# Fourier layer of a hybrid diffusion block on Trainium2: sixteen operand buffers, gate rows ahead of the last transposes, the transform's sums on VectorE

## The chip, the cores and the metric

The kernel runs on one core of one Trainium2 chip. The metric is the time of one execution on the device, in microseconds (us). Three executions of the kernel before took 2755.8, 2761.44 and 2761.8 us; their median is 2761.44 us. The profiled execution took 2763.41 us, of which the profile's span covers 2761.6 us.

## The reference

Two layers work on 2048 latent tokens of width 1024, with 256 context tokens. Layer 0 is attention and is not touched, apart from two loads at its start. Its output projection and the Fourier layer after it are what the change rearranges:

```python
def fourier_layer(x, shift, scale, gate, norm_g, w_in, w_out):
    h = modulate(x, norm_g, shift, scale)
    u, g = jnp.split(h @ w_in, 2, axis=-1)
    uf = u.reshape(b, n, F_GROUPS, F_GROUP_DIM)          # 4 groups of 256 channels
    f = jnp.fft.fft2(uf, axes=(1, 3), norm="ortho").real.reshape(b, n, F_WIDTH)
    return x + gate * ((f * jax.nn.silu(g)) @ w_out)
# ... and the final rms_norm(x, final_g)
```

All is in fp32 to a close tolerance, so every product is made of three matmuls of split operands: a high part (fp32r) and the rest (high by high, low by high, high by low).

## The kernel before

The helper `mm3` (L58 to L60) issues such a triple; `split` (L49, L51, L54) makes the two parts: a cast on ScalarE or GpSimd, and a subtraction on VectorE (or GpSimd). The program goes through these stages:

- **Projections and attention** (to about 2007 us). The order on TensorE, VectorE and ScalarE inside attention is written out by hand. At its start SyncE's queue loads keys and values; the helper around L685 also loads raw output weights (`wol`, 256 KB each), which are split later between attention's steps.
- **Output projection 0 and second norm** (L769 to L856). For each of four groups of 512 tokens, eight operands u are formed, multiplied with resident weights (`w0h`, `w0l`), and added to x; for each block of 128 tokens `second_mod` normalises, transposes (`tr`, eight 128x128 transposes on TensorE), modulates and stores h to memory.
- **Fourier in-projection** (L862 to L1005). The work comes as eight products named by a key: gates G0, G3, G1, G2 (one for each group of 512 tokens; 192 matmuls of 512 columns each), and E0, O0, O1, E1, the even and odd folds of two token groups times the Fourier weights (O: 96 matmuls of 512 columns; E: 192 of 258 columns). Each product has eight operands h of 512 tokens, in two halves of four. The halves lie in sets of four buffers; `SETS` says which sets a product uses. There are three sets, a, b and c, that is 12 buffers. Weights come in quarters: a raw quarter (`wraw`, two buffers) is loaded by SyncE's queue, `whi` is cast by GpSimd (whose queue also mends one column of each folded operand, L916 to L922) and `wlo` subtracted by VectorE (five buffers each). Raw operands (`hraw`) have four buffers. A gate product has two halves of weights, so there are eleven changes of weights from the first product to the last.
- **Transform** (L1030 to L1094). The DFT over positions as products with cosine and sine tables (`ch`, `cl`, `sh`, `sl`), in two halves r of the output positions and four channel groups g, 24 matmuls of 256 or 258 columns for each; then sums: `g1` to `g4` on VectorE (L1072 to L1075), FM on VectorE (L1077), FL on GpSimd (L1078). The Nyquist rows Y (`pn`) come last in each half. `x` and `y` are working copies; tables for r=0 are loaded before O1, those for r=1 after E1.
- **Output projection 1 and final norm** (L1099 to L1144). All weights `w1h`, `w1l` are loaded; then for each group of tokens eight products u of FM or FL with a gate (`gl`, three buffers), the first row of four of them replaced through `gy`, `uy` and a small DMA `u<-uy`, split into `uh` and `ul`, and four blocks of 24 matmuls for each half of the columns.

A tile scheduler orders what is outside attention: it emits instructions in an order of its own and each engine's queue runs in order. SyncE's queue issues loads in order too; a load that waits for a buffer holds up those behind it.

Of the kernel before, what the change touches and what calls it, by code (L numbers as in the profile page):

```python
# [10 lines left out]
F32 = mybir.dt.float32  # L11
F32R = mybir.dt.float32r
# [23 lines left out]
NDFT = 514  # L36
# [3 lines left out]
SETS = {"G0": "ab", "G3": "ca", "E0": "bc", "O0": "ac", "G1": "ba", "O1": "cb", "E1": "ac", "G2": "ba"}  # L40
# [49 lines left out]
def block_kernel(ctx: ExitStack, tc: tile.TileContext, a):  # L90
# [29 lines left out]
    eo_d = [dt_(f"eo{ci}", [4, P, CW]) for ci in range(2)]  # L120
    s1_d = [dt_(f"s1r{g}", [4 * NG, P]) for g in range(NG)]
# [361 lines left out]
    with ExitStack() as ph:  # L483
# [191 lines left out]
        def split_weights():  # L675

            if wraw:
                l, i, lo = wraw.pop()
                hi = wop.tile([P, 512], F32R, name="woh", tag="woh")
                split(nc, hi, lo, lo.bitcast(F32), Q, Q)  # L680
                for dst, t in zip(wo_d[l], (hi, lo)):
                    ld(dst[i], t.bitcast(F32))
            for l, i, src in wouts:
                lo = wop.tile([P, 512], F32R, name="wol", tag="wol")
                ld(lo.bitcast(F32), src)  # L685
                wraw.append((l, i, lo))
                break
# [78 lines left out]
    def load_wres(gpool, pools, l, order):  # L766
# [3 lines left out]
        res = [[], []]  # L770
        for c in range(2):
            for kt in order:
                res[c].append([])
                for src, p in zip(wo_d[l], "hl"):
                    t = pools[c].tile([P, 512], F32R, name=f"w{l}{p}{kt}{c}", tag=f"{p}{kt}{c}", bufs=1)
                    ld(t.bitcast(F32), src[c * KT + kt])
                    res[c][-1].append(t)
        return res, gate

    def out_proj(pp, lp, us, wg, x, add):  # L780

        w, gate = wg
        for c in range(2):
            cs = slice(c * 512, (c + 1) * 512)
            for i in range(4):
                ps = pp.tile([P, 512], F32, name="mm", tag="mm", bufs=5)
                ts_ = slice(i * P, (i + 1) * P)
                for k in range(KT):
                    mm3(nc, ps, us[k][0][:, ts_], us[k][1][:, ts_], *w[c][k], k == 0, k == KT - 1)
# [6 lines left out]
    with ExitStack() as ph:  # L796
        pp = ph.enter_context(tc.tile_pool(name="p3ps", bufs=2, reuse_waits="tile", space=PSUM))

        up = ph.enter_context(tc.tile_pool(name="p3u", bufs=10, reuse_waits="tile"))
        w1p = ph.enter_context(tc.tile_pool(name="p3w1", bufs=1, reuse_waits="tile"))  # L800
        xp = ph.enter_context(tc.tile_pool(name="p3x", bufs=5, reuse_waits="tile"))
        lp = ph.enter_context(tc.tile_pool(name="p3l", bufs=2, reuse_waits="tile"))
        wp = ph.enter_context(tc.tile_pool(name="p3w", bufs=1, reuse_waits="tile", side="right"))
        op = ph.enter_context(tc.tile_pool(name="p3o", bufs=4, reuse_waits="tile", side="right"))
        fp = ph.enter_context(tc.tile_pool(name="p3f", bufs=2, reuse_waits="tile", side="right"))
        wres = load_wres(lp, (wp, w1p), 0, range(KT))

        def second_mod(x, t):

            xn = lp.tile([P, D], F32, name="xn2", tag="xn2")  # L810
            ln_rows(x, xn, xn)
            for b in range(2):
# [9 lines left out]

        for g in TOKEN_GROUPS:
# [30 lines left out]
            for i in out_proj(pp, lp, us, wres, xs, Q):  # L854
                st(x1_d[4 * g + i], xs[i])
                second_mod(xs[i], 4 * g + i)  # L856


    with ExitStack() as ph:
        dp = ph.enter_context(ExitStack())  # L860
# [6 lines left out]
        O4 = sp.tile([P, 4], F32, name="O4")  # L867
        tb = dp.enter_context(tc.tile_pool(name="tab0", bufs=1, reuse_waits="tile"))
        alt = tb.tile([P, NDFT], F32, name="alt")

        def load_tables(pool, r):
            c0, w = DFT_CH[r]
            out = []
            for nm in ("ch", "cl", "sh", "sl"):
                t = pool.tile([P, 4, w], F32R, name=f"{nm}{r}")
                Q.dma_start(out=t, in_=a["dft_" + nm][:, c0:c0 + w].rearrange("(j p) n -> p j n", p=P))
                out.append(t)
            return out

        with ExitStack() as pb:  # L880
            pp = pb.enter_context(tc.tile_pool(name="p4ps", bufs=4, reuse_waits="tile", space=PSUM))
            wp = pb.enter_context(tc.tile_pool(name="p4w", bufs=2, reuse_waits="tile", side="right"))
            rp = pb.enter_context(tc.tile_pool(name="p4r", bufs=4, reuse_waits="tile", side="right"))
            hp = pb.enter_context(tc.tile_pool(name="p4g", bufs=4, reuse_waits="tile", side="right"))
            cp = pb.enter_context(tc.tile_pool(name="p4c", bufs=4, reuse_waits="tile"))
            wk = pb.enter_context(tc.tile_pool(name="p4k", bufs=2, reuse_waits="tile"))
            zp = pb.enter_context(tc.tile_pool(name="p4z", bufs=1, reuse_waits="tile"))
            h34 = zp.tile([P, KT], F32, name="h34")
            h4 = zp.tile([P, KT], F32, name="h4")
            h4h, h4l = [zp.tile([P, KT], F32R, name=nm) for nm in ("h4h", "h4l")]  # L890

            def operand(src, kt, key):

                b = SETS[key][kt // 4]
                t = (cp if b == "c" else hp).tile([P, 2, G], F32R, name="hl" + b, tag="hl" + b)
                split(nc, t[:, 0, :], t[:, 1, :], src, S)
                return t[:, 0, :], t[:, 1, :]

            def load_raw(g, kt):
                raw = rp.tile([P, G], F32, name="hraw", tag="hraw")  # L900
                ld(raw, h2_d[:, kt, g * G:(g + 1) * G])
                return raw

            def load_h2(g, key):
                return [operand(load_raw(g, kt), kt, key) for kt in range(KT)]

            def load_fold(half, op, key):

                out = []
                for kt in range(KT):  # L910
                    a_, b_ = [load_raw(g, kt) for g in TOKEN_GROUPS[2 * half:2 * half + 2]]
                    e = wk.tile([P, G], F32, name="hf", tag="hf")
                    V.tensor_tensor(out=e, in0=a_, in1=b_, op=op)  # L913
                    if op is ALU.add or half == 0:

                        Q.tensor_copy(e[:, 0:1], a_[:, 0:1])  # L916
                        if half == 0 and op is ALU.add:
                            Q.tensor_copy(h34[:, kt:kt + 1], b_[:, 0:1])
                    else:

                        Q.tensor_tensor(out=e[:, 0:1], in0=b_[:, 0:1], in1=h34[:, kt:kt + 1], op=ALU.subtract)
                        Q.tensor_tensor(out=h4[:, kt:kt + 1], in0=b_[:, 0:1], in1=h34[:, kt:kt + 1], op=ALU.add)  # L922
                    out.append(operand(e, kt, key))
                return out

            def load_w4(ci):

                w = CW if ci == 0 else 512
                ph_, pl_ = [], []
                for q in range(4):  # L930
# [331 lines left out]
```

## Time and profile before

| | |
|---|---|
| median of three executions | 2761.44 us |
| profiled execution, its span | 2763.41 us, 2761.6 us |
| TensorE (PE) busy | 2588.6 us, 94% of the span |
| VectorE (DVE), ScalarE (ACT), GpSimd (POOL) busy | 1828.6, 1394.0, 1110.6 us |
| TensorE idle 2187 to 2762 us, largest | for `uh` 13.1, `whi` 10.3, `xn` 9.8, `hla` 8.4 us |

A busy TensorE is not TensorE at its peak: a matmul of 512 columns shows as 0.39 us, and the next starts 0.23 us after it, since they overlap. Where the granted clock falls to one half, the same matmuls start 0.43 us apart and TensorE still counts as busy. So the time lost in a stage is read as its length less the number of matmuls times the undisturbed spacing of their starts.

### The profile page before, as it was taken

How to read it: one execution, taken by the hardware profiler on the slowest of the kernel's cores; microseconds unless marked ns; L12 is line 12 of the kernel's file. 1: busy time of each engine (PE TensorE's matmuls, PEld its weight loads, DVE VectorE, ACT ScalarE, POOL GpSimd, SP SyncE). 2: the span in 40 equal slices, each digit the busy share in tenths (PEclk: the TensorE clock that was granted, in tenths of full speed). 3: DMA queues.
4: the chain of work that ended last, by engine and by line, in shares of the span. 5: the costliest groups of instructions: out<-in, count | busy, mean ns of one | idle time of the engine just before them, and what ended most of it. 6: DMA issues, size and time to landing. Idle time of an engine off the chain costs nothing. (4 is left out here: it accounts for less than half of the span.)

```text
span 2761.6 us, 44905 instructions
## 1 busy us (share of the span) xinstructions
PE 2588.6 (94%) x15209; PEld 2248.2 (81%) x15209; DVE 1828.6 (66%) x3959; ACT 1394.0 (50%) x3704; POOL 1110.6 (40%) x1024
## 2 busy tenths in 40 slices
PE   4889999999987999999999999999899899989798
PEld 2668887787875999999999999999878777778687
DVE  6663643756406888888888888888864534464565
ACT  3531221512215888888888888888733422221112
POOL 3221331233315996655556555566412322242000
PEclk7899999999998999999999999999999999999899
DMA  9456555466426441310151012100396766664542
GB/s 298 124 153 184 159 170 185 125 185 189 146 94 224 162 158 46 100 32 29 32 167 32 30 31 79 33 30 26 126 322 222 234 200 215 209 200 155 181 142 92
DMA packets 305621, 380.96 MB, mean 138 GB/s; under 512 B 27920, under 2 KB 188384, under 8 KB 305392
## 3 DMA queue, kind: packets, MB, share of 16 engines
q1 hardware_dynamic: 166544, 275.77, 31.3%
q10 hardware_dynamic: 133664, 93.38, 11.0%
q0 software_dynamic: 5184, 8.93, 1.1%
q8 instruction: 122, 2.00, 0.3%
q14 instruction: 107, 0.88, 0.1%
HBM read 259.39 MB, written 118.55 MB: 137 GB/s over the span
## 5 line engine op out<-in xcount | busy, mean ns | idle before, releaser
L551 DVE TENSOR_REDUCE m<-s 128x1 f32<-128x512 f32 (+1 forms) x960 | 579.7, 633 | 185.9 <-PE s L543 177.8
L563 ACT ACTIVATE e<-s,nm 128x512 f32<-128x512 f32 (+1 forms) x960 | 615.2, 654 | 68.8 <-DVE nm L555 65.5
L647 ACT CAST th<-ptr 128x512 fp32r<-128x512 f32 x576 | 340.6, 592 | 132.7 <-PE ptr L643 117.1
L651 DVE TENSOR_TENSOR tl<-ptr,th 128x512 fp32r<-128x512 f32 x576 | 379.1, 681 | 37.5 <-ACT th L647 37.5
L643 PE MATMUL ptr<-ident,e 128*128 128x128 f32 x2304 | 346.3, 273 | 8.3 <-DVE tl L651 6.8
L605 POOL TENSOR_TENSOR e<-e 128x768 f32<-128x768 f32 x189 | 343.0, 1847 | 0.0
L643 PEld LDWEIGHTS ptr<-ident,e 128*128 128x128 f32 x2304 | 269.9, 140 | 36.0 <-DVE tl L651 5.8
L543 PE MATMUL s<-kB,qh 128*128 128x512 f32 (+1 forms) x768 | 283.1, 378 | 7.3 <-ACT e L563 7.3
L51 POOL TENSOR_SCALAR whi<-wraw 128x1024 fp32r<-128x1024 f32 (+1 forms) x104 | 126.4, 1218 | 386.3 <-PE mm L59 156.1
L58 PE MATMUL mm<-whi,ghi 128*128 128x512 f32 x688 | 271.7, 398 | 10.5 <-DVE vvl L54 5.7
L60 PE MATMUL mm<-whi,glo 128*128 128x512 f32 x688 | 272.2, 397 | 3.5 <-DVE glo L54 3.5
L59 PE MATMUL mm<-wlo,ghi 128*128 128x512 f32 x688 | 272.3, 397 | 0.0
L602 POOL TENSOR_SCALAR e<-e,rs 128x768 f32<-128x768 f32 x192 | 170.5, 912 | 247.6 <-DVE rs L578 247.6
L543 PE MATMUL s<-kB,ql 128*128 128x512 f32 (+1 forms) x768 | 250.2, 338 | 0.0
L54 DVE TENSOR_TENSOR wlo<-wraw,whi 128x1024 fp32r<-128x1024 f32 (+1 forms) x104 | 134.6, 1297 | 166.6 <-POOL whi L51 166.6
L602 POOL TENSOR_SCALAR e<-e,c 128x768 f32<-128x768 f32 x189 | 168.7, 911 | 141.8 <-ACT e L563 82.1
L317 POOL TENSOR_TENSOR t<-qn,rope 128x256 f32<-128x256 f32 (+1 forms) x128 | 112.6, 901 | 261.5 <-issue 102.1
L563 ACT ACTIVATION_READ_ACCUMULATOR e<-s,nm 128x1 f32 x960 | 202.1, 211 | 0.0
L58 PE MATMUL pv<-th,vAh 128*128 128x256 f32 x576 | 168.7, 293 | 0.2 <-ACT oT L616 0.2
L58 PE MATMUL pv<-th,vBh 128*128 128x256 f32 x576 | 165.3, 287 | 0.0
L58 PEld LDWEIGHTS mm<-whi,ghi 128*128 128x128 f32 x688 | 130.5, 190 | 38.5 <-DVE vvl L54 6.1
L59 PE MATMUL pv<-tl,vAh 128*128 128x256 f32 x576 | 159.9, 278 | 0.0
(342 smaller groups left out, 6362.1 us busy)
## 6 DMA issues: line engine op xcount, KB each, us to landing
wraw<-in_w_in SPq DMA_DIRECT2D x56, 512.0 KB
hraw<-h SPq DMA_DIRECT2D x96, 256.0 KB
aw<-in_adaT SPq DMA_DIRECT2D x64, 256.0 KB
g<-sg ACTq DMA_DIRECT2D x64, 256.0 KB
gl<-g SPq DMA_DIRECT2D x64, 256.0 KB
wraw<-in_wg SPq DMA_DIRECT2D x64, 256.0 KB
kB<-kB SPq DMA_DIRECT2D x24, 384.0 KB
awr<-in_adaT SPq DMA_DIRECT2D x32, 256.0 KB
```

Of the source, the lines that this page charges most:

```text
L54: (lo_eng or nc.vector).tensor_tensor(out=lo, in0=src, in1=hi.bitcast(F32), op=ALU.subtract)
L58: nc.tensor.matmul(out, lh, rh, start=start, stop=False)
L59: nc.tensor.matmul(out, lh, rl, start=False, stop=False)
L60: nc.tensor.matmul(out, ll, rh, start=False, stop=stop)
L543: T.matmul(ps[:, c - o:c - o + cw], l, r[c // KP][:, k:k + cw], start=(j == 0), stop=(j == len(self.terms) - 1))
L551: V.tensor_reduce(out=self.m3[:, i:i + 1], in_=self.segs[i][:, 0:SEG[i][1]], axis=AX.X, op=ALU.max)
L563: S.activation(self.e[:, o:o + w], self.segs[i][:, 0:w], AF.Exp, bias=self.nm, accum_out=self.s3[:, i:i + 1])
L602: eng.tensor_scalar(out=self.e[:, sg], in0=self.e[:, sg], scalar1=by, scalar2=1.0, op0=ALU.mult, op1=ALU.mult)
L605: eng.tensor_tensor(out=onto[:, sg], in0=onto[:, sg], in1=self.e[:, sg], op=ALU.add)
L643: T.transpose(self.tr[:, k, i, :], self.p.es[i][:, kt * P:(kt + 1) * P], ident)
L647: S.copy(self.th, self.tr.rearrange("p k i q -> p k (i q)"))
L651: V.tensor_tensor(out=self.tl, in0=self.tr.rearrange("p k i q -> p k (i q)"), in1=self.th.bitcast(F32), op=ALU.subtract)
```

## The change

- `SETS` names four sets, a to d: 16 operand buffers. Sets b and d lie where later both halves' tables lie, which are loaded by GpSimd's queue once O1 and E1 are done with b and d.
- In output projection 0 the normalisation of a block is separated from its transposes, which come one block later; x has four buffers instead of five. The weights, raw and operand buffers of the in-projection are opened before the stage ends, and two of G0's eight row blocks stand ahead of the last block's transposes.
- In the transform Y comes first in each half, the FL sums move to VectorE, small copies to ScalarE, and the alternating term of the odd part moves into the sine table's row 0 (no `O4`). Row 0 of FL is replaced by Y once, by four small DMAs (and row 0 of FM by Y later, for group 2), in place of 16 loads `gy` and 16 `u<-uy`.
- In output projection 1 the first group's operands are loaded between the two halves of the weights; `gl` has five buffers; for the first group the loops are exchanged, operand by operand over four accumulators (`by_row`).
- Two of the raw output weights at attention's start wait for a VectorE copy that stands at a later step.

```diff
-SETS = {"G0": "ab", "G3": "ca", "E0": "bc", "O0": "ac", "G1": "ba", "O1": "cb", "E1": "ac", "G2": "ba"}
+SETS = {"G0": "ac", "G3": "db", "E0": "cd", "O0": "ab", "G1": "cd", "O1": "ab", "E1": "cd", "G2": "ac"}
...
                 lo = wop.tile([P, 512], F32R, name="wol", tag="wol")
+                if l == 0 and i < 2:
+                    V.tensor_copy(lo[:, 0:1], ones[:, 0:1])
                 ld(lo.bitcast(F32), src)
...
+            acc = [pp.tile([P, 512], F32, name="mm", tag="mm", bufs=bufs) for _ in range(4 if by_row else 0)]
+            for k in range(KT if by_row else 0):
+                for i in range(4):
+                    ts_ = slice(i * P, (i + 1) * P)
+                    mm3(nc, acc[i], us[k][0][:, ts_], us[k][1][:, ts_], *w[c][k], k == 0, k == KT - 1)
...
             for i in out_proj(pp, lp, us, wres, xs, Q):
                 st(x1_d[4 * g + i], xs[i])
-                second_mod(xs[i], 4 * g + i)
+                if normed:
+                    second_mod(*normed)
+                normed = norm(xs[i], 4 * g + i)
...
+        first = gates(TOKEN_GROUPS[0], "G0")
+        next(first)
+        next(first)
+        second_mod(*normed)
+        for _ in first:
+            pass
+        pa.close()
...
-            t = (cp if b == "c" else hp).tile([P, 2, G], F32R, name="hl" + b, tag="hl" + b)
+            t = (hpr if b in "ac" else hpl).tile([P, 2, G], F32R, name="hl" + b, tag="hl" + b)
...
-                e1 = rp.tile([P, G], F32, name="eo", tag="hraw")[:, 0:w]
+                e1 = gk.tile([P, 512], F32, name="eo", tag="sg")[:, 0:w]
...
-            tabs.append(load_tables(tb1, 1))
+            for r, (c0, w) in enumerate(DFT_CH):
+                tabs.append([tb.tile([P, 4, w], F32R, name=f"{nm}{r}") for nm in ("ch", "cl", "sh", "sl")])
+                for t, nm in zip(tabs[r], ("ch", "cl", "sh", "sl")):
+                    Q.dma_start(out=t, in_=a["dft_" + nm][:, c0:c0 + w].rearrange("(j p) n -> p j n", p=P))
...
-                        S.copy(y, m[:, 1, :])
...
-                        V.scalar_tensor_tensor(out=y, in0=al, scalar=O4[:, g:g + 1], in1=m[:, 1, :],
-                                               op0=ALU.mult, op1=ALU.add)
+                    S.copy(y, m[:, 1, :])
...
-                        Q.tensor_tensor(out=FL[:, g, k, rs], in0=g3[:, 0:256], in1=g4[:, 0:256], op=op)
+                        V.tensor_tensor(out=FL[:, g, k, rs], in0=g3[:, 0:256], in1=g4[:, 0:256], op=op)
...
+                        ld(FL[0:1, g, :, :], Y[g:g + 1, :, :])
...
-                gt = gp.tile([P, G], F32, name="gl", tag="gl")
+                gt = gp.tile([P, G], F32, name="gl", tag="gl", bufs=5)
...
-                if b >= 4:
-                    ld(u[0:1, :], uy[b - 4:b - 3, :])
...
+        load_c, gate = load_wres(lp, (wp, w1p), 1, KORDER)
+        w0 = load_c(0)
+        us = operands(0)
+        ld(a0_d, FM[0:1].rearrange("p g k n -> p (g k n)"))
+        wres = [w0, load_c(1)], gate
```

On TensorE, the end of output projection 0 and the start of G0 stood so before (`w0` are output weights, `xn` a normalised block, `hla` an operand of G0):

```order
L59 MATMUL mm<-w0l_25078,uh 128x512
L815 MATMUL tr<-ident,xn_26857 128x128 x4
L60 MATMUL mm<-w0h_25076,ul 128x512
L815 MATMUL tr<-ident,xn_26857 128x128 x4
L815 MATMUL tr<-ident,xn_26924 128x128 x8
L815 MATMUL tr<-ident,xn_26991 128x128 x8
L58 MATMUL mm<-hla,whi 128x512
```

In the changed kernel the last two blocks' transposes stand among G0's products:

```order
L59 MATMUL mm<-w0h_25079,ul 128x512
L57 MATMUL mm<-hla,whi 128x512
L58 MATMUL mm<-hla,whi 128x512
L59 MATMUL mm<-hla,wlo 128x512
L834 MATMUL tr<-ident,xn_26860 128x128 x4
...
L834 MATMUL tr<-ident,xn_26927 128x128 x8
...
L834 MATMUL tr<-ident,xn_26994 128x128 x4
L57 MATMUL mm<-hla,whi 128x512
L834 MATMUL tr<-ident,xn_26994 128x128 x4
```

The last block but two's transposes moved behind one triple and two, the next block's behind about ten, the last block's behind sixteen. On SyncE's queue, the loads from the transform to the first group of output projection 1 stood so before (`w1h` weights of the second half, `gl` gates):

```order
L1120 DMA gl<-g_100 128x512
L776 DMA w1h_30115<-wo1h 128x512
...
L776 DMA w1l_30145<-wo1l 128x512
L1105 DMA fing<-in_final_g 128x1024
L1113 DMA gy<-g_98 1x512
...
L1120 DMA gl<-g_97 128x512
L1136 DMA xr<-x_103 128x1024
...
L1128 DMA u<-uy 1x16x32 x2
```

They now stand so:

```order
L1147 DMA gl<-g_96 128x512
L1122 DMA F_29629<-Y_29631 1x4x1
...
L1120 DMA FL<-Y 1x16x64
L1147 DMA gl<-g_100 128x512
L1147 DMA gl<-g_97 128x512
...
L1147 DMA gl<-g_101 128x512
L779 DMA w1h_30186<-wo1h 128x512
```

All eight gates of the first group now come ahead of the weights' second half, and no `gy` or `u<-uy` is among them. On GpSimd the tables of both halves moved behind the fifth of G2's eight weight casts:

```order
L53 TENSOR_TENSOR E1L<-eo,E1H 128x258 x8
L50 TENSOR_SCALAR whi<-wraw 128x2x512 x4
L1057 DMA ch_29647<-in_dft_ch 128x4x258
...
L1057 DMA sl_29658<-in_dft_sl 128x4x256
L50 TENSOR_SCALAR whi<-wraw 128x2x512 x3
```

Before, the four of r=1 stood among the `E1L` and ahead of seven casts.

## Rows read from the trace of the kernel before

**Rows 1.** TensorE's waits, 2187 to 2762 us: in total, times, longest (us)
```profile
PE mm L58 <- ACT uh L49: 13.1, 1, 13.1
PE mm L58 <- POOL whi L51: 10.3, 6, 3.4
PE tr L815 <- DVE xn L210: 9.8, 4, 6.4
PE mm L58 <- ACT hla L49: 8.4, 4, 6.1
```

**Rows 2.** Busy time by stage: length, PE, PEld, DVE, ACT, POOL, PE clock, DMA share, GB/s
```profile
2194.50:2212.50 18.00, 8.24 (x44) 6.79 (x44) 9.54 (x27) 11.28 (x31) 4.51 (x5) 0.79 0.76 226
2212.50:2523.00 310.50, 288.65 (x1412) 237.80 (x1411) 137.33 (x176) 72.29 (x132) 87.25 (x109) 0.97 0.63 197
2523.00:2554.00 31.00, 27.23 (x217) 24.87 (x216) 23.17 (x56) 4.01 (x10) 12.60 (x20) 1.00 0.58 194
2554.00:2580.00 26.00, 10.04 (x23) 7.23 (x24) 10.58 (x20) 2.28 (x4) 3.96 (x4) 0.61 0.81 285
2580.00:2752.00 172.00, 172.00 (x746) 139.95 (x744) 107.80 (x242) 37.04 (x73) 0.00 (x0) 1.00 0.38 118
```

**Rows 3.** TensorE's timeline: undisturbed matmuls of 512 and of 256 columns
```profile
2220.00 0.40 PE L58 MATMUL mm<-hla,whi 128*128 128x512 f32 x1
2220.23 0.40 PE L59 MATMUL mm<-hla,whi 128*128 128x512 f32 x1
...
2549.88 0.28 PE L59 MATMUL ae<-cl,E1H 128*128 128x256 f32 x1
2550.00 0.28 PE L60 MATMUL ae<-ch,E1L 128*128 128x256 f32 x1
```

**Rows 4.** TensorE's timeline at the end of output projection 0
```profile
2208.01 1.94 PE L815 MATMUL tr<-ident,xn 128*128 128x128 f32 x8 [6.37 <-DVE xn L210]
2210.89 1.94 PE L815 MATMUL tr<-ident,xn 128*128 128x128 f32 x8 [0.94 <-DVE xn L210]
```

**Rows 5.** TensorE's timeline: the longest wait at a change of weights
```profile
2285.40 0.50 PE L58 MATMUL mm<-hlc,whi 128*128 128x512 f32 x1 [3.43 <-POOL whi L51]
```

**Rows 6.** SyncE's queue: raw operands in G0; gates in the transform
```profile
2271.75 9.85 SPq L901 DMA_DIRECT2D hraw<-h  x8
2535.32 17.65 SPq L1120 DMA_DIRECT2D gl<-g  x6
...
2569.95 1.21 SPq L1128 DMA_DIRECT2D u<-uy  x2
```

**Rows 7.** GpSimd's timeline ahead of the cast in rows 5
```profile
2284.16 0.18 POOL L918 COPY h<-hraw 128x1 f32<-128x1 f32 x1 [3.13 <-DMA hraw<-h]
```

**Rows 8.** TensorE's timeline at the start of output projection 1
```profile
2557.54 0.79 PE L60 MATMUL mm<-w1h,ul 128*128 128x512 f32 x1 [2.46 <-DVE ul L54]
...
2576.51 0.79 PE L58 MATMUL mm<-w1h,uh 128*128 128x512 f32 x1 [13.13 <-ACT uh L49]
```

**Rows 9.** FM sums, 2523 to 2562 us: busy us, mean ns of one, idle before
```profile
L1077 DVE TENSOR_TENSOR FM<-g,g 128x256 f32<-128x256 f32 x16 | 9.0, 593 | 0.0
```

**Rows 10.** VectorE's timeline in the transform: a sum, and two pairs of FM
```profile
2541.42 0.41 DVE L1074 TENSOR_TENSOR g<-x,bo 128x258 f32<-128x258 f32 x1
2541.75 1.30 DVE L1077 TENSOR_TENSOR FM<-g,g 128x256 f32<-128x256 f32 x2
...
2545.36 0.74 DVE L1077 TENSOR_TENSOR FM<-g,g 128x256 f32<-128x256 f32 x2
```

**Rows 11.** Start of attention: SyncE's queue, then TensorE's first scores
```profile
817.84 0.82 SPq L685 DMA_DIRECT2D wol<-in_w_out  x2
...
829.32 0.77 PE L543 MATMUL s<-kAh,qh 128*128 128x512 f32 x1 [8.79 <-issue]
```

**Rows 12.** A table's load: GpSimd's timeline at its issue
```profile
2473.46 0.78 POOL L876 DMA_DIRECT2D sl<-in_dft_sl  x1
```

**Rows 13.** The same load: KB, us from issue to landing
```profile
sl<-in_dft_sl POOLq DMA_DIRECT2D x1, 512.0 KB, 9.6
```

More of the change, by code (lines that the diff above doesn't have):

```diff
@@ new lines, in load_w4 @@
+        def load_w4(ci):
+            w = CW if ci == 0 else 512
+            ph_, pl_ = [], []
+            for q in range(4):
+                raw = wp.tile([P, 2, CW], F32, name="wraw", tag="wraw", bufs=2)[:, :, 0:w]
+                for k in range(2):
+                    kt = 2 * q + k
+                    if ci < 2:
+                        ld(raw[:, k, :], wur_d[kt][:, ci * CW:ci * CW + w])
+                    else:
+                        ld(raw[:, k, :], a["wg2"][kt * P:(kt + 1) * P, (ci - 2) * 512:(ci - 1) * 512])
+                hi = wp.tile([P, 2, CW], F32R, name="whi", tag="whi", bufs=5)[:, :, 0:w]
+                lo = wp.tile([P, 2, CW], F32R, name="wlo", tag="wlo", bufs=5)[:, :, 0:w]
+                split(nc, hi, lo, raw, Q)
+                ph_ += [hi[:, 0, :], hi[:, 1, :]]
+                pl_ += [lo[:, 0, :], lo[:, 1, :]]
+            return ph_, pl_
@@ new lines, in gates @@
+        def gates(g, key):
+            hs = [operand(load_raw(g, kt), kt, key) for kt in range(KT)]
+            for ci in (2, 3):
+                whi, wlo = load_w4(ci)
+                for i in range(4):
+                    ps = pp.tile([P, 512], F32, name="mm", tag="mm", bufs=5)
+                    ms = slice(i * P, (i + 1) * P)
+                    for kt in range(KT):
+                        mm3(nc, ps, whi[kt][:, ms], wlo[kt][:, ms], *hs[kt], kt == 0, kt == KT - 1)
+                    o = gk.tile([P, 512], F32, name="sg", tag="sg")
+                    S.activation(o, ps, AF.Silu)
+                    st(g2_d[(ci - 2) * 4 + i][:, g * G:(g + 1) * G], o)
+                    yield
@@ new lines, in gates_all @@
+        def gates_all(g, key):
+            for _ in gates(g, key):
+                pass
+        gates_all(TOKEN_GROUPS[1], "G3")
+        project(0, 0, load_fold(0, ALU.add, "E0"))
+        project(1, 0, load_fold(0, ALU.subtract, "O0"))
+        gates_all(TOKEN_GROUPS[2], "G1")
+        odd_ = load_fold(1, ALU.subtract, "O1")
+        split(nc, h4h, h4l, h4)
+        project(1, 1, odd_)
+        project(0, 1, load_fold(1, ALU.add, "E1"))
+        gates_all(TOKEN_GROUPS[3], "G2")
+        pb.close()
@@ L1024, in block_kernel @@
         FL = fp.tile([P, 4, 2, 512], F32, name="FL")
[L1025 to L1026 removed]
+        F4 = [[fp.tile([P, 4], F32, name=f"F4{b}{c}") for c in range(2)] for b in range(2)]
         Y = fp.tile([4, 2, 512], F32, name="Y")
@@ L1132, in block_kernel @@
                 us.append((h, l))
+            return us
+        load_c, gate = load_wres(lp, (wp, w1p), 1, KORDER)
[3 more added lines that the diff above has]
+        wres = [w0, load_c(1)], gate
+        fing = lp.tile([P, D], F32, name="fing", tag="fing")
+        ld(fing, a["final_g"].partition_broadcast(P))
+        for g in range(NG):
+            if g:
+                us = operands(g)
             xs = []
```

330 lines of the change are left out of this document (141 added, 189 removed).

## The prediction

> **What bounds the kernel now.** I read the stages first, then TensorE's waits, then its timeline at the longest of them, then the queues of the engine that released each. The reader should see in the waits [rows 1] that four releasers make up 41.6 us after 2187 us, and in the stages [rows 2] that all of it lies before 2580 us: from there to 2752 us TensorE is busy 172.00 of 172.00 us. TensorE is the bound, so a stage's loss is its length less its matmuls times their undisturbed spacing: 0.23 us from start to start for 512 columns and 0.12 for 256 [rows 3]. That counts the clock as well, which idle time costs: the granted clock was 0.79 and 0.61 in the two disturbed stretches and 1.00 around them [rows 2].
>
> Three stretches lose time.
>
> *End of output projection 0*, 2194.5 to 2212.5 us: 18.0 us. The order shows 12 matmuls left (2.7 us) and 32 transposes; eight take about 0.8 us at full clock (my estimate from 1.94 us at half clock, overlap taken off), so 3.2 us. Work is some 6, loss 12.0 us. TensorE stands 6.37 and 0.94 us for the normalised block [rows 4], with nothing else in its order.
>
> *In-projection*, 2212.5 to 2523 us: 310.5 us. 960 matmuls of 512 columns at 0.23 us are 221, 432 of 258 columns at 0.12 are 52, small products 2: 275. Loss 36 us: 21.9 us idle (310.5 less 288.65), and most of the rest 3% of clock [rows 2]. The places are changes of weights, the longest wait 3.43 us [rows 5], and E1's operands, one wait of 6.1 us of 8.4 [rows 1]. Before the first, SyncE's queue held eight raw operands for 9.85 us, waiting for buffers [rows 6], and GpSimd stood 3.13 us for one of them, with the late cast `whi` next in its queue [rows 7]: operands that find no buffer hold up weights behind them. E1's operands stood in set a, which the product just ahead of it still used.
>
> *Transform and start of output projection 1*, 2523 to 2751.9 us: 228.9 us. 216 matmuls at 0.12 are 25.9, 768 at 0.23 are 176.6: 202.5. Loss 26.4 us. 13.13 us is one wait for `uh` and 2.46 one for `ul` [rows 8]. Behind the first lies SyncE's queue, which stood 17.65 us at six `gl` loads with three buffers, so that half of the weights, then `gy`, then `u<-uy` at 2569.95 us came late [rows 6].
>
> **The change part by part.**
>
> *Attention's start.* Two loads of 256 KB leave the head of SyncE's queue; the first scores come 11.5 us after them, after an idle 8.79 us [rows 11]. At the 285 GB/s of a stretch dense with loads [rows 2] 0.5 MB is 1.8 us; some of it lies beside work that ends later anyway. I take 1.3 us, bounds 0 and 3. The copy they wait for is one column on VectorE, covered.
>
> *Transposes one block later, two G0 rows ahead.* 16 triples (11 us) now lie between the output weights' end and the last block's transposes. Blocks came at 2208.01 and 2210.89 us [rows 4], about 7 and 10 us after the weights' end; the order asks for them 7 and 11 us after it. So the 12.0 us fill with G0's work, if its weights and operands are there. Their loads now come ahead of the stage's end; the raw operand buffers are four, x buffers fall from five to four, and the last x load sits between raw operands, so a quarter of weights can be 3 to 5 us late. Residual 3 us, bounds 1 and 9: gain 9.
>
> *Sixteen buffers.* E1 (sets c, d) no longer follows a product on the same set except through G1, a whole O1 (22 us) earlier, so most of the 8.4 us for `hla` goes. For weight changes nothing is added to `whi`, `wlo` or `wraw` (5, 5, 2): what helps is that operands find buffers sooner, so that weights behind them on SyncE's and GpSimd's queues stand free. Following the eleven changes through both queues in the new order with durations of this trace, I find each raw quarter issued 0 to 2 us before it must be. That is thin, so I leave a third of the loss: 12 us, bounds 2 and 25. Gain 24. Where this cover goes, the next thing late is again the cast `whi`, then E1's stored halves, which now have two buffers instead of four and load in the same queue.
>
> *Tables.* Eight loads, 4.2 MB, stand on GpSimd's queue behind the fifth of G2's eight casts. Issuing one holds GpSimd 0.78 us [rows 12], so 6.2 us, between a cast that is early by half of G2 and one that must wait for a buffer of the first half's last row block. I cost them at nothing. The last of four landed after 9.6 us [rows 13]; twice the bytes, by the same row, 19 us, ends before G2's end if issued in G2's first half. The Trainium skill has a rule against me here, in "DMA: Bandwidth & Descriptors", section "Issuing engines are not separate DMA queues": transfers share the same 16 engines whoever issues them, so a second queue gives the tables no room of their own. The slow 9.6 us for 0.5 MB beside SyncE's loads agrees; it is a rival below.
>
> *Transform.* VectorE takes 16 FL sums, loses four `y` sums. A sum takes 0.41 us and the next starts 0.33 after it; a pair of FM 0.74 us alone and 1.30 beside GpSimd's FL [rows 10], on average 0.593 us each [rows 9]. With GpSimd silent I take 0.335 for each: r=0, a group is nine of them, 3.02 us, against TensorE's 24 x 0.12 = 2.88; r=1, eight, 2.68; Y five more, 1.7 us. Sum 24.5 us against TensorE's 25.9, so the two run level. After the last matmul VectorE has some of the last group's sums left, and `ul` of the first operand, whose FM was done long before, so output projection 1 starts about 1.4 us after TensorE's end, 27.3 us after the stage's start. By the mean of [rows 9] it would be slower: a rival. The Trainium skill speaks to it in "SBUF — State Buffer", section "Who interferes with whom": a VectorE instruction with two SBUF inputs contends with a GpSimd instruction that reads SBUF. By the rule the inflated sums go with GpSimd's; by the mean they stay. The two FM rows agree with the rule.
>
> *First group of output projection 1.* With `by_row` TensorE needs an operand each 12 x 0.2275 = 2.73 us; VectorE makes one in 1.3 us (u and ul, each twice a sum's columns, 0.66: an estimate from the same rows). Gates are all in SyncE's queue ahead of the second half of the weights, which has 4 x 8 x 3 x 0.2275 = 22 us of matmuls to land 4.2 MB (6.3 MB at 285 GB/s). `gl` with five buffers no longer stands 17.65 us. Row 0 by four loads of Y replaces 16 `u<-uy` and 16 `gy`; they wait for FL of the last group, 26 us in, with the second half's last weights behind them, needed 49 us in. Residual 3 us, bounds 1.5 and 9: gain 23.4.
>
> *Rest.* The saved and restored row 0, the alternating row in a table, copies on ScalarE (4.01 busy in 31 us [rows 2]): nothing, up to 1 us.
>
> Sum: 1.3 + 9 + 24 + 23.4 = 57.7 us. The profiled execution took 2763.4 us, 1.8 of it outside the span, and stands 2.0 us above the median of the runs: 2763.4 - 57.7 = 2705.7, on the median's scale 2703.7. I say 2704.
>
> **Rivals.**
>
> 1. *Forecast*, 2704; its own range 2692 to 2716. Chance 0.60.
> 2. *Weights stay late.* The eleven changes keep about what they lost, since `wraw` has two buffers and operands still share both queues with them, or G0 starts without its weights: the in-projection keeps 25 of 36 us and the projection's end 6 of 12. 2704 + 13 + 3 = 2720, between 2714 and 2730. For it: six waits for `whi` [rows 1] are more than those for operands. Against: [rows 6, 7], where the weights' lateness comes from the operands ahead. 0.22.
> 3. *VectorE becomes the transform's bound.* If its sums cost 0.593 us, 73 of them are 43 us against 27.3, 16 us late; with half the inflation 8. 2704 + 9 = 2713, to 2720. Against it: [rows 10], 0.74 for a pair alone. 0.09.
> 4. *Tables late.* If the shared engines give them and G2's last weights 19 us from G2's second half on, while SyncE already loads `w1h`, the transform starts up to 15 us later: 2719. For it: 9.6 us for one [rows 13], a DMA share of 0.63 through the whole in-projection [rows 2]. 0.04.
> 5. *Slower: every change of weights waits.* Through the added buffers operands are asked for earlier, and if their eight raw loads stand in the queue ahead of each quarter, each of the eleven changes waits for its last quarter some 6 us (the 9.85 us that eight raw loads held the queue [rows 6], less the 4 us that three quarters of a last row block of 24 matmuls leave), and the clock, at half for as long as in [rows 2], gives up 1.5 more: 82 us where 36 were lost. Then 2704 + 82 - 12 = 2774. It decides from 6.3 us a change, 70 us in all. The longest so far is 3.43 [rows 5]. 0.04.
> 6. *The change doesn't do what it says*: the scheduler orders loads so that the waits keep their places, 2755 to 2762. 0.01.
>
> **How the numbers follow.** About 0.2%, 5.5 us, is what a measurement of this kernel can tell from no change. Forecast and rivals 2 to 4 are all faster by more: 0.95. Within it lie rival 6 and part of 5: 0.02. Slower, the rest of 5: 0.03. The range takes rivals 1 to 4 in with their bounds, down to all residuals at their lower bounds (2 + 10 + 1.5 us better, 1.7 more at attention: 2689): 2688 to 2731.
>
> **What would show it.** In the changed profile the wait for `uh` after the transform should be under 2 us and no SyncE load of `gl` stand over 5 us; the granted clock should be 1.00 from 2195 to 2690 us apart from a few tenths; waits for `hla` should be gone and those for `whi` under 8 us in total; FM and FL pairs on VectorE should take 0.74 us; transposes should stand between G0's matmuls without a wait over 1.5 us; scores should start near 828 us. I am wrong if `whi` is a larger wait than before, if TensorE waits on `g` or `x` in the transform for more than 3 us, or if the first matmul of G0 waits for its weights.

## The result and the profile after

The changed kernel took 2721.4 us (median of four executions, 2719.19 to 2730.51) where the kernel before took 2761.62 us on the same chip (2755.8 to 2768.7): a ratio of 0.9859, with a 95% interval of 0.9827 to 0.9892. It is faster by 40 us, inside the stated range, but 17 us above the likeliest time and outside that case's own 2692 to 2716. It came out where rival 2 stood (2720). The profiled execution took 2719.19 us, its span 2717.3, 44.2 us less than before's.

The stages, from the first and last instruction of each on TensorE (us):

| | before | after | gain | forecast |
|---|---|---|---|---|
| start to the first output weights' matmul | 2007.5 | 2005.2 | 2.3 | 1.3 |
| from there to the transform's start | 515.5 | 493.7 | 21.9 | 9 + 24 |
| transform's start to the last matmul | 229.0 | 209.5 | 19.5 | 23.4 |
| behind the last matmul | 9.5 | 9.0 | 0.5 | 0 |

The stages of the changed kernel (columns as in [rows 2]) answer to that group:

```profile
2187.00:2198.50 11.50, 9.30 (x38) 7.52 (x37) 9.60 (x18) 4.03 (x12) 3.57 (x3) 0.85 0.68 234
2198.50:2498.80 300.30, 285.67 (x1427) 236.94 (x1427) 143.84 (x189) 80.03 (x156) 89.95 (x112) 0.98 0.67 210
2498.80:2525.70 26.90, 25.88 (x218) 24.91 (x216) 23.67 (x67) 8.40 (x33) 0.00 (x0) 1.00 0.72 241
2525.70:2536.00 10.30, 6.99 (x20) 5.07 (x21) 8.39 (x19) 2.80 (x5) 0.00 (x0) 0.67 0.99 330
2536.00:2707.00 171.00, 171.00 (x744) 139.43 (x744) 104.27 (x235) 37.42 (x72) 0.00 (x0) 1.00 0.43 142
```

The 11.8 us from the last output weights' matmul to G0's first (2200.7 to 2212.5 us before) are down to 0.2, the transform is at TensorE's pace, and the last 171 us are as full as before. But the in-projection still leaves TensorE 14.6 us idle, and its waits from 2187 us on (total, times, longest) say for what:

```profile
PE mm L57 <- POOL whi L50: 7.5, 4, 4.3
PE mm L57 <- DVE g L1110: 3.3, 1, 3.3
PE mm L58 <- DVE wlo L53: 2.4, 1, 2.4
PE tr L834 <- DVE xn L210: 2.2, 1, 2.2
PE mm L59 <- DVE wlo L53: 2.0, 2, 1.4
PE qtr L982 <- DVE row L1017: 1.6, 1, 1.6
PE mm L57 <- ACT uh L48: 1.0, 1, 1.0
PE mm L57 <- POOL hf L970: 0.8, 1, 0.8
```

Against [rows 1], the 13.1 us for `uh` are 1.0 and the 8.4 us for `hla` have gone; the waits for weights, `whi` and `wlo`, are 11.9 us and have not. (`hf` is the mend that ended just behind a cast in GpSimd's queue; its waits are counted with those for weights below.) In TensorE's timeline G0 starts with the last output weights' matmul, ahead of the transposes, and a new wait stands at the second accumulator of output projection 1:

```profile
2198.31 0.39 PE L59 MATMUL mm<-w0h,ul 128*128 128x512 f32 x1
2198.54 0.39 PE L57 MATMUL mm<-hla,whi 128*128 128x512 f32 x1
...
2199.25 0.60 PE L834 MATMUL tr<-ident,xn 128*128 128x128 f32 x4
...
2525.65 0.50 PE L57 MATMUL mm<-w1h,uh 128*128 128x512 f32 x1 [1.02 <-ACT uh L48]
...
2530.19 0.79 PE L57 MATMUL mm<-w1h,uh 128*128 128x512 f32 x1 [3.31 <-DVE g L1110]
```

VectorE's timeline there shows what came ahead of that sum, L1110 of the last channel group: `ul` of three operands and, from 2528.78 us, one `u` of the projection.

```profile
2525.63 0.69 DVE L53 TENSOR_TENSOR ul<-u,uh 128x512 fp32r<-128x512 f32 x1
2526.24 0.75 DVE L1113 TENSOR_TENSOR FL<-g,g 128x256 f32<-128x256 f32 x2
2526.91 1.29 DVE L53 TENSOR_TENSOR ul<-u,uh 128x512 fp32r<-128x512 f32 x2
...
2529.72 0.41 DVE L1110 TENSOR_TENSOR g<-m,y 128x256 f32<-128x256 f32 x1
```

SyncE's queue (answering to [rows 6]) stands 3.22 us at the gates, but still 15.34 us at raw operands, now O1's, ahead of a quarter of G1's weights:

```profile
2330.75 15.34 SPq L896 DMA_DIRECT2D hraw<-h  x9
2346.18 0.86 SPq L910 DMA_DIRECT2D wraw<-in_wg  x2
...
2509.31 3.22 SPq L1147 DMA_DIRECT2D gl<-g  x5
```

GpSimd got that quarter at 2352.89 us, and TensorE waited 4.29 us for its cast. That looked like the forecast's mechanism at work once more, so it was tested first.

### The profile page after: what moved, and what is told of

The parts are those of the page before. It is cut to its first block, busy times and chain, and to the rows that moved or that the text cites. A ratio compares the mean times of both kernels' runs of the same rounds, so it can differ in the third digit from the quotient of the medians.

```text
span 2717.3 us, 44829 instructions
## 1 busy us (share of the span) xinstructions
PE 2582.7 (95%) x15201; PEld 2247.9 (83%) x15201; DVE 1825.5 (67%) x3963; ACT 1396.9 (51%) x3726; POOL 1092.6 (40%) x1000
## 4 chain that ended last, share of the span: by engine, by line
PE 62%; DMA 6%; DVE 3%; ACT 1%; issue 1%; POOL 1%; SPq 0%; ACTq 0%; DVEq 0%; POOLq 0%
PE s L543 17%; PE ptr L643 9%; PE mm L57 6%; PE mm L59 6%; PE mm L58 6%; PE pv L57 5%; PE pv L59 5%; PE pv L58 5%; DMA hraw<-h 2%; DVE m L551 1%; DMA wraw<-in_wg 1%; DMA gl<-g 1%; DMA eo<-eo 1%; DMA g<-sg 1%; DMA kAl<-kAl 0%
```

## The experiments

Each kernel was timed against the kernel before on its own chip; the change itself stands at 0.9859 there. Two stretches of the profiles are compared: A, from the first output weights' matmul to the transform's start (before 515.5, changed 493.7 us), and B, from there to the last matmul (229.0, 209.5 us). Three profiles whose program is the same in A gave 493.7, 496.8 and 495.8 us, two others 499.5 and 493.1: one profile of A is good to 3 us in the first and 6 in the second program. B repeats within 1 us. A holds output projection 0 as well, which most edits leave alone. The in-projection by itself, from G0's first matmul to the transform's start, took 300.3 us in the change, 302.0 and 300.2 in the other two profiles of its program (310.5 before), and their waits for `whi`, `wlo` and `hf` come to 12.7, 13.5 and 14.4 us. Where an edit is in the in-projection, its own length is given too.

**Three sets of buffers.**

```diff
-SETS = {"G0": "ac", "G3": "db", "E0": "cd", "O0": "ab", "G1": "cd", "O1": "ab", "E1": "cd", "G2": "ac"}
+SETS = {"G0": "ac", "G3": "da", "E0": "cd", "O0": "ad", "G1": "ca", "O1": "dc", "E1": "ad", "G2": "ca"}
```

> The changed kernel with three sets of operand buffers again (the assignment of before, with its a, b, c on the new a, c, d; set b stands empty); all else is the change. If the buffers are what took time out of the in-projection (theory: operands that find no buffer hold weights and E1's start up), the in-projection is 8 to 12 us longer than the changed kernel's 300.3, E1 waits again about 6 us for its operands, and the whole is about 2730. If the buffers did nothing (rival: the gain in the in-projection is that of G0's early rows alone), the time stays at 2719 to 2723.

Ratio 0.9864 (0.9846 to 0.9882), A 495.9 us: no loss that can be told there. The in-projection is 305.4 us, 3 to 5 more than with four sets, and its waits for `whi`, `wlo` and `hf` are 16.2 us. TensorE's waits there name no operand of E1:

```profile
PE mm L57 <- POOL whi L50: 8.7, 7, 2.8
PE mm L58 <- DVE wlo L53: 4.1, 1, 4.1
PE mm L57 <- POOL hf L970: 2.9, 1, 2.9
```

So the fourth set, the change's headline, gained 5 us at most of the 24 that were forecast, and a set too few was not why E1 had waited.

**Weights by GpSimd's queue; operands by ScalarE's queue.** The loads of `wraw` or of `hraw` leave SyncE's queue:

```diff
...
-                        ld(raw[:, k, :], a["wg2"][kt * P:(kt + 1) * P, (ci - 2) * 512:(ci - 1) * 512])
+                        Q.dma_start(out=raw[:, k, :], in_=a["wg2"][kt * P:(kt + 1) * P, (ci - 2) * 512:(ci - 1) * 512])
...
-            ld(raw, h2_d[:, kt, g * G:(g + 1) * G])
+            S.dma_start(out=raw, in_=h2_d[:, kt, g * G:(g + 1) * G])
```

> The changed kernel with the in-projection's raw weights loaded by GpSimd's queue in place of SyncE's. Theory: of the 22 us that the in-projection still loses, most is weights that stand behind raw operands in SyncE's queue (nine of them for 15.3 us ahead of a quarter that TensorE then waits 4.3 us for); with a queue of their own the waits for whi and wlo fall from 13 us to under 5 and the whole to about 2708 to 2712. Rival: the DMA engines are full there (share 0.91 at 2320 to 2340 us), so that the weights land as late from any queue: 2718 to 2724, or later by what issuing costs on GpSimd.

> The changed kernel with the raw operands loaded by ScalarE's queue, the weights alone (with the stored halves) on SyncE's. By the theory of the queue's order the waits for whi fall as with the weights on GpSimd, to a whole of 2708 to 2714, unless ScalarE, which stands at a load whose buffer is not free, casts operands late: then waits for hl tiles take the place of those for whi and the time stays above 2718. By the rival (full DMA engines) nothing changes: 2718 to 2724.

0.9846 (0.9823 to 0.9868) with A 494.5, and 0.9856 (0.9837 to 0.9875) with A 499.8 us; the in-projection 304.6 and 304.5 us. The waits for `whi`, `wlo` and `hf` are 15.4 and 15.7 us where the change has 12.7. So SyncE's order is not by itself what makes the weights late. The two runs don't clear in-order queues, though. In the first, 4.5 of the 15.4 us are one wait at 2484.49 us for a quarter of G2 that the edit had put beside the tables in GpSimd's queue; it landed 14.0 us after its issue. And both leave the casts where they were, in GpSimd's queue behind the mends. In the second run TensorE waited 3.27 us, until 2348.42, for a cast that ran right behind a mend, which had waited for an operand:

```profile
2346.72 0.19 POOL L974 TENSOR_TENSOR h<-hraw,h 128x1 f32<-128x1 f32 x1 [1.87 <-DMA hraw<-h]
2346.87 1.50 POOL L50 TENSOR_SCALAR whi<-wraw 128x1024 fp32r<-128x1024 f32 x1
```

**Transposes in their old place, then a PSUM pool of its own.**

```diff
...
-                if normed:
-                    second_mod(*normed)
-                normed = norm(xs[i], 4 * g + i)
+                second_mod(*norm(xs[i], 4 * g + i))
...
+        pa.close()
+        pp = pb.enter_context(tc.tile_pool(name="p4ps", bufs=4, reuse_waits="tile", space=PSUM))
```

The first edit alone (with the early row blocks and their transposes undone) is the first run, both edits the second.

> The changed kernel with each block's transposes right behind its normalisation, and G0 wholly behind the last of them, as before. By the prediction's step this gives back 9 us (8 to 11): about 2730, with two waits for xn of about 6 and 1 us ahead of G0. The rival, that G0's weights and operands are late anyway and the early rows only fill what G0 would lose later, gives 2720 to 2724.

0.9869 (0.9847 to 0.9891), A 497.0 us, within the spread. The scheduler put G0's triples among the transposes all the same.

> The kernel of the run without early gates (transposes right behind each normalisation), and besides the in-projection has a PSUM pool of its own, opened when output projection 0's is closed, as before; in its order all transposes stand ahead of G0 again. Theory after the first runs: not where the source puts the transposes, but the shared PSUM pool lets G0 start among them. Then from the first output weights' matmul to the transform's start it takes 8 to 12 us more than the 493.7 of the changed kernel (504), with waits for xn of about 6 and 1 us, and the whole is about 2733. Rival, that early pools of buffers in SBUF do it: as without early gates, 497.

0.9903 (0.9884 to 0.9922), A 511.5 us, 14.5 to 18 more. The old order and the old wait are back, at half clock behind it (0.43 us from start to start):

```profile
2214.27 1.94 PE L834 MATMUL tr<-ident,xn 128*128 128x128 f32 x8 [5.06 <-DVE xn L210]
2217.15 1.94 PE L834 MATMUL tr<-ident,xn 128*128 128x128 f32 x8 [0.94 <-DVE xn L210]
2219.07 0.77 PE L57 MATMUL mm<-hla,whi 128*128 128x512 f32 x1
...
2220.05 0.63 PE L59 MATMUL mm<-hla,wlo 128*128 128x512 f32 x1
2220.48 0.63 PE L57 MATMUL mm<-hla,whi 128*128 128x512 f32 x1
```

So the pool did it: the in-projection takes its PSUM tiles from output projection 0's. With a pool of its own its first product stood, in the order, behind the last transposes. The edit also closes output projection 0's other buffers earlier, but G0 did not lack operands or weights: this run's fifth quarter was ready 15 us ahead of G0's first product.

```profile
2203.13 1.22 DVE L53 TENSOR_TENSOR wlo<-wraw,whi 128x1024 fp32r<-128x1024 f32 x1
```

**A third raw weight buffer; four, four and four.** In the first, `wraw` has three buffers and output projection 0's operands nine; in the second `wraw`, `whi` and `wlo` have four each in the change's memory:

```diff
-                raw = wp.tile([P, 2, CW], F32, name="wraw", tag="wraw", bufs=2)[:, :, 0:w]
+                raw = wp.tile([P, 2, CW], F32, name="wraw", tag="wraw", bufs=4)[:, :, 0:w]
...
-                hi = wp.tile([P, 2, CW], F32R, name="whi", tag="whi", bufs=5)[:, :, 0:w]
+                hi = wp.tile([P, 2, CW], F32R, name="whi", tag="whi", bufs=4)[:, :, 0:w]
...
```

> The changed kernel with three raw weight buffers in place of two (room for it from output projection 0's operands, nine of each in place of ten). Theory: with two, the last quarter's load at a change of weights can start only when TensorE has released a whi, GpSimd has cast and VectorE subtracted; load 4.0 to 4.5 us, cast 1.05 and subtraction 1.2 stand in series, and a load of 6 us or more is late whatever queue issues it. With three all are loaded ahead: waits for whi and wlo fall from 12 us to under 4, the in-projection from 300.3 to about 291, the whole to about 2712. Rival, that the DMA engines are full at these places: the waits stay above 9 us and the time at 2718 to 2724.

0.9835 (0.982 to 0.985), A 492.6 us: waits for weights 9.9 us, the in-projection 292.9 us without a loss of clock, 7 to 9 less than the change; but output projection 0, whose operands had lost a buffer, took 199.8 us where the change's program took 193.4 to 195.6. Between the two theories.

> The changed kernel with four raw weight buffers, four whi and four wlo in place of two, five and five: the same memory, nothing taken from output projection 0. By the theory that a load stands in series at each change of weights, all of a product's raw quarters are now loaded ahead and only cast and subtraction (2.25 us) stand between TensorE's release of a quarter and its next use 4.1 us after; waits for whi and wlo fall under 5 us, no clock is lost in the in-projection, and from the first output weights' matmul to the transform it takes 484 to 488 us in place of 493.7: about 7 us faster than the change on the same chip. Rival, that GpSimd and VectorE are late with cast and subtraction for other work in their queues: the waits stay at 8 to 12 us, only their places move, and the fifth buffers' loss adds to them.

0.985 (0.983 to 0.9869), A 499.5 us, the in-projection 302.1; waits for weights 14.4 us, at fewer places. With every quarter's load free to go early they did not fall. Since `whi` and `wlo` lost a buffer each, this doesn't exclude a shortage of raw weight buffers. It bears out the rival. O0's four quarters were issued by 2305.24 us, the last four loads landing 5.2 to 5.5 us after issue, but GpSimd cast the first of them at 2323.09, right behind the last of eight mends. Each of these mends an operand that VectorE has first to fold from two raw ones. TensorE, done with E0 at 2321, waited for the cast:

```profile
2303.25 2.23 SPq L908 DMA_DIRECT2D wraw<-wur  x4
...
2322.94 0.10 POOL L970 MEMSET hf<- 128x1 f32 x1 [2.22 <-ACT eo L1000]
2323.09 4.12 POOL L50 TENSOR_SCALAR whi<-wraw 128x1024 fp32r<-128x1024 f32 x3
...
2324.38 0.96 PE L57 MATMUL mm<-whi,hla 128*128 128x512 f32 x3 [3.34 <-POOL whi L50]
```

So weights that have landed still wait for operands, in GpSimd's queue.

**Stored halves in the raw operands' buffers.**

```diff
-                    e1 = gk.tile([P, 512], F32, name="eo", tag="sg")[:, 0:w]
+                    e1 = (gk.tile([P, 512], F32, name="eo", tag="sg") if half == 0 else rp.tile([P, G], F32, name="eo", tag="hraw"))[:, 0:w]
```

> The changed kernel with the stored halves of O1 and E1 loaded into the raw operands' four buffers again, as before (in the change they have the gates' two). Theory: in the kernel before, these twelve loads took buffers from E1's and G2's raw operands, and that, not the missing fourth set, made TensorE wait 8.4 us for E1's operands; then waits for hl tiles of 4 to 8 us at E1 or G2 come back and the whole is 2725 to 2730. Rival, that the wait came from sets of operands alone: 2718 to 2724 with no such wait.

0.9853 (0.9836 to 0.9869), A 497.9 us, the in-projection 305.5. E1's wait for its operands is back:

```profile
PE mm L57 <- POOL whi L50: 8.5, 4, 4.0
PE mm L57 <- ACT hlc L48: 7.3, 2, 4.8
```

That is the wait of [rows 1], 8.4 us: its cause was the four raw buffers that O1's and E1's stored halves took. In A it shows little, since waits for weights fell as it rose (`whi`, `wlo` and `hf` 9.9 us).

**FL on GpSimd, three gates.**

```diff
-                        V.tensor_tensor(out=FL[:, g, k, rs], in0=g3[:, 0:256], in1=g4[:, 0:256], op=op)
+                        Q.tensor_tensor(out=FL[:, g, k, rs], in0=g3[:, 0:256], in1=g4[:, 0:256], op=op)
...
-                gt = gp.tile([P, G], F32, name="gl", tag="gl", bufs=5)
+                gt = gp.tile([P, G], F32, name="gl", tag="gl")
```

> The changed kernel with the transform's FL sums on GpSimd again. By the prediction's rows FM pairs then take 1.30 us in place of 0.74 (8 x 0.56 = 4.5 us more) and VectorE loses 16 x 0.335 = 5.4 us of FL: level within 1 us on VectorE, with FL ready 1 to 2 us later, so from the transform's start to the last matmul 209 to 213 us in place of 209.5, the whole 2719 to 2726: the move by itself gained next to nothing. Rival, that it is what shortened the transform: 5 us or more longer, and TensorE waits for sums in the transform.

0.9851 (0.9836 to 0.9866), B 208.6 us: no longer. FM sums are slow again beside GpSimd's FL; in the changed kernel, both on VectorE, each takes 0.42 us. First this run's two groups (busy, mean ns, idle before), then the change's:

```profile
L1112 DVE TENSOR_TENSOR FM<-g,g 128x256 f32<-128x256 f32 x16 | 11.1, 732 | 0.0
...
L1113 POOL TENSOR_TENSOR FL<-g,g 128x256 f32<-128x256 f32 x16 | 14.3, 917 | 33.8 <-DVE g L1110 33.8
```

```profile
L1112 DVE TENSOR_TENSOR FM<-g,g 128x256 f32<-128x256 f32 x16 | 6.0, 416 | 0.0
L1113 DVE TENSOR_TENSOR FL<-g,g 128x256 f32<-128x256 f32 x16 | 6.0, 418 | 0.0
```

VectorE saves 5.1 us on FM and takes 6.0 on for FL: a move that about pays for itself and no more. The Trainium skill ("SBUF — State Buffer", section "Who interferes with whom") has VectorE instructions with two SBUF inputs contend with GpSimd instructions that read SBUF; 0.73 against 0.42 us agrees.

> The changed kernel with three gl buffers in place of five, all else as changed. If SyncE's standing at the gates (17.65 us before) is what cost the start of output projection 1, from the transform's start to the last matmul it takes 5 us or more longer than 209.5. Rival, the row-0 path (gy, uy, u<-uy, gone here) alone made the 13.13 us wait: the weights' second half is needed only 24 us after the first matmul, so the time stays within 2 us of 209.5.

0.9861 (0.9839 to 0.9883), B 209.6 us: no loss, so two of the five buffers are not needed. But the queue's stand of 17.65 us in [rows 6] did not come back with three: the longest at the gates, with other loads and weights between them now, was 2.82 us. Whether that stand was the price is not tested.

```profile
2528.16 2.82 SPq L1147 DMA_DIRECT2D gl<-g  x2
```

**Every second PSUM bank.** On top of four, four and four:

```diff
-            acc = [pp.tile([P, 512], F32, name="mm", tag="mm", bufs=bufs) for _ in range(4 if by_row else 0)]
+            acc = [pp.tile([P, 512], F32, name="mm", tag="mm", bufs=bufs) for _ in range(8 if by_row else 0)][::2]
```

> The run with four, four and four, and for output projection 1's first group four accumulators in every second of eight PSUM banks. In the changed kernel TensorE waits 3.31 us there for a transform sum before its second accumulator. Theory: that accumulator's bank is the one that the last channel group's products still hold; every second bank was released a group earlier, so the 3.31 us and the 2 us of clock behind it go, and from the transform's start to the last matmul it takes 204 to 206 us in place of 209.5. Rival, that the wait covers all banks whichever is taken: 209 to 210.5.

0.9834 (0.9817 to 0.9851), but B 209.6 us with the same wait of 3.31 us: the theory of that one bank falls. A is 493.1 us with the program that had 499.5 above, so its ratio is no gain of the edit.

**Half the raws of the odd folds.** This run leaves work out: O0 and O1 take one token group for both, so the folds that they multiply are zeros.

```diff
-                a_, b_ = [load_raw(g, kt) for g in TOKEN_GROUPS[2 * half:2 * half + 2]]
+                a_ = load_raw(TOKEN_GROUPS[2 * half], kt)
+                b_ = load_raw(TOKEN_GROUPS[2 * half + 1], kt) if alu is ALU.add else a_
```

> The changed kernel in which the odd folds O0 and O1 load one raw operand in place of two and take it for both (so what they compute is not the fold): 16 loads of 256 KB fewer, 4.2 MB, half of them beside E0 and O0, half beside G1 and O1; every instruction on the engines stays. Theory left after the other runs: neither the queue nor the number of raw weight buffers, but the transfers themselves are short there (DMA share 0.87 to 1.00 in the stretches ahead of the waits); then the waits for whi, wlo and hf fall from 12.7 us to under 6, and from the first output weights to the transform it takes 483 to 488 us in place of 493.7, the whole 0.980 to 0.983 of the kernel before. Rival, that casts and subtractions stand behind other work on GpSimd and VectorE: the waits stay above 9.5 us and the time within 3 us of the change's, 0.985 to 0.987.

0.9822 (0.9801 to 0.9843), A 484.2 us, 9.5 less than the change's profile and 11 less than the mean of the three; the in-projection 292.1, 8 to 10 less. Waits for `whi`, `wlo` and `hf` are 6.9 us:

```profile
PE mm L57 <- POOL whi L50: 3.5, 4, 1.8
PE mm L58 <- DVE wlo L53: 2.1, 1, 2.1
...
PE mm L57 <- POOL hf L971: 1.3, 1, 1.3
```

In the changed kernel the DMA share (last but one column) stands at 0.87 to 0.94 in four of five stretches ahead of its worst waits, from E0 to G1:

```profile
2290.00:2300.00 10.00, 9.18 (x76) 8.94 (x75) 7.09 (x9) 2.44 (x5) 3.12 (x5) 1.00 0.87 289
2300.00:2310.00 10.00, 10.00 (x86) 10.00 (x85) 5.83 (x7) 3.45 (x8) 1.24 (x3) 1.00 0.94 313
2310.00:2320.00 10.00, 10.00 (x62) 8.95 (x61) 7.06 (x9) 4.54 (x9) 3.07 (x6) 1.00 0.74 221
2320.00:2330.00 10.00, 8.52 (x37) 6.58 (x37) 6.62 (x9) 3.89 (x7) 2.23 (x2) 1.00 0.93 307
2330.00:2340.00 10.00, 9.88 (x44) 7.67 (x42) 3.32 (x6) 2.35 (x5) 2.28 (x5) 1.00 0.91 256
```

So the weights come sooner where fewer operands are loaded. The Trainium skill ("DMA: Bandwidth & Descriptors", section "Issuing engines are not separate DMA queues") says that transfers run on the same 16 engines whoever issues them; the two runs that moved loads to another queue agree, with 304.6 and 304.5 us, though they left the casts' queue as it was. The run does not part the bytes from the operand buffers and queue slots that go with them. Against bytes alone speaks that the five stretches moved 221 to 313 GB/s, where 2400 to 2410 us of the same profile moved 360, and that an in-projection as short, 292.9 us, came from a third raw weight buffer with every byte loaded. For the raw operands' four buffers speaks what SyncE's operand loads waited for from 2300 to 2360 us in the changed kernel: mostly VectorE's fold and GpSimd's mend, which free a buffer.

```profile
SPq L896 <- DVE hf L962: 14.9, 10, 3.5
SPq L896 <- POOL hf L973: 7.2, 2, 4.0
...
SPq L896 <- DMA hraw<-h: 3.8, 5, 1.7
```

More buffers for raw operands, or casts ahead of the mends in GpSimd's queue, were not run.

No run is clearly faster than the change with its work whole: those with the lowest ratios (0.9834, 0.9835) have intervals that overlap the change's, and in A (493.1 and 492.6 us) lie 1 us below its spread.

## Why the prediction was right or wrong

**Direction and range: right.** Each of the three stretches that lost time lost less.

**Transposes and G0: right in mechanism, under-sized.** Forecast 9 us; undoing it costs 14.5 to 18 (A 511.5 against 497.0 and 493.7). The step credited the source's new order; it is the shared PSUM pool. And it counted the loss only up to G0's first matmul, while in the run with its own pool the granted clock was 0.50 for 4.2 us more, inside G0: some 2 us. The rest of what it missed is not explained.

**Sixteen buffers: wrong, the step that missed most.** In the profiles the gain is 44.2 us where 57.7 were forecast; 11 of the 13.5 us are missing in A, though the transposes gave more than forecast there. The step gave 24 us to operands that find buffers sooner. With the pool undone, A is 511.5 against 515.5 and the in-projection 304.1 against 310.5: everything else in the in-projection together is worth some 4 to 6 us. One statement failed outright: "E1's operands stood in set a, which the product just ahead of it still used". O1 stood between, and the wait was for raw buffers that stored halves held. The other, "operands that find no buffer hold up weights behind them", read from [rows 6, 7], is at work still, as the rows of the runs above show. What failed is that the fourth set gives those operands their buffers. It holds operands that are already split, while late ones wait for one of four raw buffers, and the change has no more of these than the kernel before. So the waits for weights did not fall (11.0 us for `whi` and `wlo` before, 11.9 after). Whether raw buffers, the transfers or the casts' place behind the mends is the shortest of the three stays open. The DMA share of 0.63 in [rows 2] hid how dense the transfers are in places: it is a mean over 310 us with stretches above 0.9.

**Rival 2: the right time, in part by luck.** It left the in-projection a loss of 25 us, and some 23 remain (300.3 us less 275 of products and 2.4 of transposes that moved in); but it also left 6 us at the end of output projection 0, which are gone, and the transform's stretch gained 4 us less than it took over from the forecast. Of its reason, that operands share both queues with the weights is borne out for GpSimd's queue; two raw weight buffers are neither shown nor excluded.

**Transform: right, and rival 3 fell.** VectorE stayed level with TensorE; output projection 1 began 26.8 us after the transform's start (forecast 27.3). The FL move was counted as an aid, but is neutral.

**Start of output projection 1: mis-sized.** Residual forecast 3 us, measured 7.0 (209.5 less 202.5): 1.0 for `uh`, 3.31 for the last group's sums and 2 of clock behind them. The step looked at how fast VectorE makes operands, not at what its queue puts behind them. What brought the 19.5 us is not parted: FL's place and the number of the gates' buffers are excluded, so there remain the vanished `gy` and `u<-uy` loads, the operands' new place ahead of the weights, `by_row`, and the 5.6 us that VectorE no longer waits at the transform's start. These were not run.

**Tables: right.** The last landed 16.5 us after its issue at 2469.89, 12 us before the transform.

**Attention's start: not shown.** The scores started at 819.94 us, not near 828. The first output weights' matmul stood at 2005.2 us in the change's profile, but at 2006.9 to 2013.8 in the twelve runs with the same start, and at 2007.5 before.

## What to carry to other kernels

When weights come late, follow one of them from its load's issue and landing to its cast, through every in-order queue that it passes: moving its load to another queue leaves the cast behind whatever stands ahead of it on the casting engine. Ask which buffer the late loads themselves wait for before crediting another one, and look at transfers in 10 us slices just ahead of the wait, not at a stage's mean. Where one stage's first product could fill another's tail, see which pool its PSUM tiles come from; separate pools can set an order that no edit of the source's order undoes. And when work is moved to an engine that must next feed the matmuls, read its whole queue at the hand-over.

## What was not expected of the hardware

Half-clock stretches make about a quarter of what waits cost: the changed in-projection lost 14.6 us idle and, by the records at 0.5 of the clock, about 5 us more. Starting attention earlier did not help where its keys were late: in the change's profile TensorE took its first scores 9.4 us earlier than before, ran in pieces at a granted clock of 0.65 from 817 to 875 us (0.76 before), and reached the output weights only 2.3 us earlier.
